# Two heads side by side in the two halves of the rows: sliding-window attention and mLSTM of a two-layer f32 block

## The chip, the cores and the metric

The kernel runs as one program on one core of a Trainium2 chip. The time is that of one execution on the device in microseconds; lower is better. The engines are PE (matmul; PEld is its weight load), DVE, ACT, POOL and SP, which issues DMAs. PE contracts over the partition dimension: a matmul's operands lie on up to 128 rows (partitions), and an operand of 64 rows may lie on rows 0 to 63 or on rows 64 to 127.

## The reference, cut to what matters

Two layers of feed-forward, token mixing, feed-forward and a gated embedding, then further blocks, on 512 rows of 1024. Within token mixing, these two parts matter here:

```python
# attention: 8 query heads over 2 key/value heads of 64, window 128, one sink logit per head
scores = jnp.einsum('bnqhgd,bnkhd->bnhgqk', qb, kb) * (HEAD_DIM ** -0.5)
scores = jnp.where(valid, scores, NEG_INF)
probs = jax.nn.softmax(jnp.concatenate([scores, sink], axis=-1), axis=-1)[..., :-1]
out = jnp.einsum('bnhgqk,bnkhd->bnqhgd', probs, vb)
...
# mLSTM: 4 heads of 64; C_t = f_t C_{t-1} + i_t v_t k_t^T, n_t = f_t n_{t-1} + i_t k_t,
# h_t = C_t q_t / max(|n_t . q_t|, 1), carried in a running-max (m) scaled form
h_m = mlstm_chunkwise(m_heads(q_m), m_heads(k_m), m_heads(v_m), i_pre, f_pre)
h_m = h_m * rsqrt(mean(h_m * h_m) + NORM_EPS) * mlstm_norm
y_mlstm = sigmoid(o_m) * h_m
y = jnp.concatenate([y_attn, y_mlstm, y_rwkv], axis=-1) @ w_out
```

## The kernel before

Activations are feature-major: tiles of 128 features x 512 rows of the sequence. Every weight product is a sum of three matmuls in a rounded format (operands split into a high part, names ending in h, and a low part, ending in l), accumulated in a PSUM bank named ps_ps. `mix` (once per layer) runs `lin_fm` over 22 tiles of w_mf; after each tile's 24 matmuls an evacuation function `evac` does the small work of the three token mixers. Tiles 16 to 21 are the queries, keys and values of the attention; behind tile 16 stands `ml_gates`, behind tile 21 the generator `attention` is started and then advanced by two steps in each of tiles 0 to 7, whose own work is the RWKV part; tiles 8 to 15 are the mLSTM's. Last come `ml_core` and the w_out product, whose operands are ymh and yml.

A scheduler of the framework orders each engine's instructions ahead of time; each engine then runs its queue in that order and waits at semaphores. PSUM has eight banks. In `mix`, `ps` has banks 0 and 1, `rw` 2 to 4, `at` 5 to 7; a call of `self.ps(shape, tag)` takes the tag's next bank in turn.

`attention` (L1072) loops over 4 blocks of 128 rows and, in each, over 4 steps i. A step is one half e of the rows (one key/value head; e = i // 2) and two of its query heads: scores of q and k over 64 rows (f32, each matmul two records in a profile) and the mask added by a bf16 product with an identity (m, id), the row maximum (mx), exponentials (pr, with their sum dn), the sink's exponential es, transposes of pr, a copy to pT, the product with v, and the division. A block's last step transposes the output (oo) back. Block 0 has 128 keys, the others 256.

`ml_gates` (L943) makes the gate rows: 16 rows x 512 (4 heads, each repeated 4 times) by scans, then splits them into Gh and Gl.

`ml_core` (L999) loops over 4 heads. Head h has its 64 features on rows 0 to 63 or 64 to 127 of tile j = h // 2. For each of four column blocks c (512, 384, 256, 128 columns wide) it broadcasts a gate row by two products of a selecting column `sel` with Gh and Gl over 16 rows, adds the triangular mask, takes the exponential (wt), multiplies k by q over 64 rows (mq in the profile, f32, two records), and multiplies both into pt. Ten products with va (64 columns and a column of ones) give the head's output; a chain of small ops (md, hh, msq, mms and the inverse root mly) normalises it. After each second head the two are transposed (hh), weighted (myg) and split (ymh, yml).

Of the kernel before, what the change touches and what calls it, by code (L numbers as in the profile page):

```python
# [10 lines left out]
F32 = mybir.dt.float32  # L11
# [46 lines left out]
NC1 = C_ROT + 128  # L58
# [8 lines left out]
def mixer_constants():  # L67
    c = np.zeros((P, NC1), np.float32)
    m = np.zeros((P, NM), np.float32)
    i = np.arange(P)  # L70
    m[:, M_UPS:M_UPS + P] = i[:, None] < i[None, :]
    m[:, M_UPI:M_UPI + P] = i[:, None] <= i[None, :]
    for n in range(7):
        b = 1 << n
        q = (i[:, None] // (2 * b) == i[None, :] // (2 * b)) & (i[:, None] % (2 * b) >= b) & (i[None, :] % (2 * b) < b)
        m[:, M_LEV + n * P:M_LEV + (n + 1) * P] = q
        if n == 0:
            m[:, M_LEV1T:M_LEV1T + P] = q.T
# [6 lines left out]
    cm = np.zeros((16, T), np.float32)  # L85
    for r in range(16):
        cm[r] = t >= P * (r // 4)
# [12 lines left out]
    return c, ca, c2, m, cm  # L100
# [11 lines left out]
class K:  # L112
# [830 lines left out]
    def ml_gates(self):  # L943
# [23 lines left out]
        pl = self.ps([16, NB, P], "rw")  # L967
        pi = self.ps([16, NB, P], "rw")
# [9 lines left out]
        cm = self.tmp("cm")[0:16, :]  # L978
# [6 lines left out]
        for b in range(NB):  # L985
            self.tr(pc[:, 0, b, :], I[:, b * P:(b + 1) * P])
            self.tr(pc[:, 1, b, :], M[:, b * P:(b + 1) * P])
# [5 lines left out]
        Gh, Gl = (pool.tile([16, T], F32R, name=n) for n in ("Gh", "Gl"))  # L993
        self.split(G, Gh, Gl)
        self.sel = pool.tile([16, 16], F32R, name="sel")
        nc.vector.tensor_copy(out=self.sel, in_=self.ident[0:16, 0:16])
        self.ml["gates"] = ac, em, Gh, Gl

    def ml_core(self, ys):  # L999

        nc, pool, ml = self.nc, self.pool, self.ml
        ac, em, Gh, Gl = ml["gates"]
        va = ml["va"]
        small = lambda nm, sh, bufs=2: pool.tile([P] + sh, F32, tag=nm, name=nm, bufs=bufs)
        for h in range(4):
            j, o = h // 2, (h % 2) * 64
            PT = []
            for c in range(NB):
                n = T - c * P
                rr = c * 4 + h  # L1010
                pw = self.ps([P, n], "at")
                sel = bc(self.sel[:, rr:rr + 1], [16, P])
# [3 lines left out]
                w = self.tmp("wt")[:, :n]  # L1016
                nc.scalar.activation(w, pw, AF.Exp, bias=ac[:, c, rr:rr + 1])
                s = self.ps([P, n], "rw")
                self.mm(s, ml[f"k{j}"][o:o + 64, c * P:(c + 1) * P], ml[f"q{j}"][o:o + 64, c * P:])
                pt = self.tmp("pt")[:, :n]  # L1020
                nc.vector.scalar_tensor_tensor(pt, s, 0.125, w, op0=ALU.mult, op1=ALU.mult)
                PT.append(pt)
            pn = self.ps([P, NB, 65], "at")
            for b in range(NB):
                for c in range(b + 1):
                    self.mm(pn[:, b, :], PT[c][:, (b - c) * P:(b - c + 1) * P], va[:, c, h, :], c == 0, c == b)
            den = small("md", [NB])
            nc.scalar.activation(den, pn[:, :, 64], AF.Abs)
            nc.vector.tensor_max(den, den, em[:, :, h])
            nc.vector.reciprocal(den, den)  # L1030
            if h % 2 == 0:
                hh = self.tmp("hh").rearrange("p (b a d) -> p b a d", a=2, d=64)
            hv = hh[:, :, h % 2, :]
            nc.vector.tensor_mul(hv, pn[:, :, 0:64], bc(den.unsqueeze(2), [P, NB, 64]))
            sq = small("msq", [NB, 64], 1)
            nc.scalar.activation(sq, hv, AF.Square)
            ms = small("mms", [NB])
# [3 lines left out]
            nc.vector.tensor_mul(hv, hv, bc(rs.unsqueeze(2), [P, NB, 64]))  # L1041
            if h % 2:
                pt = self.ps([P, NB, P], "rw")
                for b in range(NB):
                    self.tr(pt[:, b, :], hh[:, b, :, :].rearrange("p a d -> p (a d)"))
                yg = self.tmp("myg")
                nc.vector.scalar_tensor_tensor(yg, pt.rearrange("p a b -> p (a b)"), self.v(f"mnorm{self.l}", j), ml[f"og{j}"], op0=ALU.mult, op1=ALU.mult)
                self.split(yg, *ys[6 + j])
# [23 lines left out]
    def attention(self):  # L1072
# [5 lines left out]
        for j in range(4):  # L1078
            at[f"o{j}"] = at[f"q{j}"]
        for b in range(NB):  # L1080
# [3 lines left out]
            for i in range(4):  # L1084
                e, j0 = i // 2, 2 * (i % 2)
                o = slice(e * 64, e * 64 + 64)
                sc = self.ps([P, 2, 256], "at")
                for g in range(2):
                    ks = slice((b - 1 + k0) * P, (b + 1) * P)
                    dst = sc[:, g, k0 * P:]  # L1090
                    self.mm(dst, QT[j0 + g][o, sl], KT[o, ks], True, False)
                    self.mm(dst, self.id16, self.m16[:, k0 * P:256], False, True)
                mx = small("mx", [2])
                nc.vector.tensor_reduce(mx, sc[:, :, k0 * P:], axis=AX.X, op=ALU.max)
                sk = rb[:, so + 4 * e + j0:so + 4 * e + j0 + 2]
                nc.vector.scalar_tensor_tensor(mx, mx, 0.125, sk, op0=ALU.mult, op1=ALU.max)
                nc.vector.tensor_scalar(mx, mx, -1.0, None, op0=ALU.mult)
                dn = small("dn", [2])
                pr = self.tmp("pr").rearrange("p (a b) -> p a b", b=256)
                for g in range(2):  # L1100
                    nc.scalar.activation(pr[:, g, k0 * P:], sc[:, g, k0 * P:], AF.Exp, bias=mx[:, g:g + 1], scale=0.125,
                                         accum_out=dn[:, g:g + 1])
                es = small("es", [2])
# [4 lines left out]
                pp = self.ps([P, 2, 2, P], "at")  # L1108
                for g in range(2):
                    for kk in range(k0, 2):  # L1110
                        self.tr(pp[:, g, kk, :], pr[:, g, kk * P:(kk + 1) * P])
                pT = self.tmp("pT").rearrange("p (a b c) -> p a b c", b=2, c=P)
                nc.vector.tensor_copy(out=pT[:, :, k0:, :], in_=pp[:, :, k0:, :])
                po = self.ps([P, 2, 64], "at")
                for g in range(2):
                    for kk in range(k0, 2):
                        self.mm(po[:, g, :], pT[:, g, kk, :], vat[:, b - 1 + kk, e * 64:(e + 1) * 64], kk == k0, kk == 1)
                nc.vector.tensor_mul(oo.rearrange("p (h d) -> p h d", d=64)[:, 2 * i:2 * i + 2, :], po, bc(dn.unsqueeze(2), [P, 2, 64]))
                if i == 3:
# [913 lines left out]
```

## Time and profile before

| what | value |
|---|---|
| median of 3 runs | 4457.08 us (4456.84 to 4468.8) |
| the profiled execution | 4456.82 us, span 4454.9 us |
| PE busy | 4207.3 us, 94% |
| DVE, ACT, POOL busy | 2642.3 us (59%), 1613.4 us (36%), 845.6 us (19%) |
| granted TensorE clock, mean of the span | 0.955 |
| attention, first layer | within 449 to 565 us of the span |
| ml_core, first and second layer | 715.9 to 781.9 and 1985.3 to 2048.3 us |

The span is the profiled part; 1.9 us lie around it. A granted clock of 1 is 2.4 GHz, 0.5 is 1.2 GHz, and a value between is a mean over a stretch that had both. Matmuls overlap their neighbours in the pipeline, so what one costs is read from start to next start rather than from its duration.

### The profile page before, as it was taken

To read this page: it belongs to the slowest core of one execution; us is meant where nothing else is said; L and a number is where in the kernel's file an instruction comes from. 1 tells how busy PE (TensorE), PEld (TensorE's weight loads), DVE (VectorE), ACT (ScalarE), POOL (GpSimd) and SP (SyncE) were. 2 spreads that over 40 slices of the span, in tenths; PEclk is the share of its full clock that TensorE was granted. 3 is DMA by queue.
4 is the path that set the end of the run, shared out by engine and by line. 5 is a ranking of instruction groups with operands and counts; after the bars stand their busy time and mean duration, and the time that the engine had idled before them with its cause. 6 is when DMAs were issued, how large, how long until landed. Compare 5 with 4: busy or idle time off the path is not lost. (4 is left out here: it accounts for less than half of the span.)

```text
span 4454.9 us, 56951 instructions
## 1 busy us (share of the span) xinstructions
PE 4207.3 (94%) x21867; PEld 3559.3 (80%) x21867; DVE 2642.3 (59%) x5019; ACT 1613.4 (36%) x2542; POOL 845.6 (19%) x739
## 2 busy tenths in 40 slices
PE   8998999999999999999999889899878889999998
PEld 7887687888888886877888768788877878888887
DVE  4435664543464445645442766645667878777876
ACT  3223422432352233323332543443323743333332
POOL 0002210100110012111000332102655024333331
PEclk9999997999999999978999899899989999999999
DMA  3233100322332231002323310333444689899895
GB/s 122 99 93 123 48 11 29 122 96 95 128 114 99 96 126 58 25 29 78 106 95 115 129 59 29 118 129 132 166 148 170 251 311 328 308 322 323 312 318 184
DMA packets 234592, 628.71 MB, mean 141 GB/s; under 512 B 26800, under 2 KB 93488, under 8 KB 229968
## 3 DMA queue, kind: packets, MB, share of 16 engines
q1 hardware_dynamic: 195008, 464.11, 30.5%
q0 software_dynamic: 38736, 159.93, 10.1%
q8 instruction: 171, 2.80, 0.3%
q10 hardware_dynamic: 576, 1.05, 0.1%
q14 instruction: 101, 0.83, 0.1%
HBM read 562.06 MB, written 62.91 MB: 140 GB/s over the span
## 5 line engine op out<-in xcount | busy, mean ns | idle before, releaser
L193 PE MATMUL ps_ps<-xh,wl 128*128 128x512 f32 (+2 forms) x3568 | 1310.2, 368 | 53.0 <-DVE wl L184 52.8
L193 PE MATMUL ps_ps<-xl,wh 128*128 128x512 f32 (+2 forms) x3568 | 1315.8, 369 | 24.3 <-DVE xl L340 23.7
L193 PE MATMUL ps_ps<-xh,wh 128*128 128x512 f32 (+2 forms) x3568 | 1306.8, 368 | 33.0 <-ACT xh L348 12.6
L183 ACT CAST wh<-st 128x1024 fp32r<-128x1024 f32 (+1 forms) x560 | 580.0, 1038 | 1409.2 <-PE ps_ps L193 977.8
L184 DVE TENSOR_TENSOR wl<-st,wh 128x1024 fp32r<-128x1024 f32 (+1 forms) x496 | 600.2, 1211 | 431.2 <-ACT wh L183 430.3
L193 PEld LDWEIGHTS ps_ps<-xh,wl 128*128 128x128 f32 x3568 | 691.0, 194 | 147.1 <-DVE wl L184 60.1
L193 PEld LDWEIGHTS ps_ps<-xl,wh 128*128 128x128 f32 x3568 | 690.3, 194 | 118.5 <-DVE xl L340 35.2
L193 PEld LDWEIGHTS ps_ps<-xh,wh 128*128 128x128 f32 x3568 | 687.8, 193 | 119.0 <-ACT xh L348 14.0
L345 POOL TENSOR_TENSOR y<-y,x 128x256 f32<-128x256 f32 x64 | 54.7, 856 | 1756.0 <-DVE y L344 1515.3
L439 DVE TENSOR_TENSOR gu<-ps_ps,R 128x512 f32<-128x512 f32 x176 | 120.9, 691 | 450.1 <-PE ps_ps L193 449.4
L193 PE MATMUL ps_ps<-mh,wl 128*128 128x512 f32 (+1 forms) x920 | 327.8, 356 | 2.5 <-DVE wl L184 2.5
L193 PE MATMUL ps_ps<-mh,wh 128*128 128x512 f32 (+1 forms) x920 | 327.4, 356 | 1.2 <-DVE kf L1499 0.9
L193 PE MATMUL ps_po<-vh,ah 128*128 128x512 f32 x768 | 303.6, 397 | 25.8 <-ACT ah L1826 20.3
L193 PE MATMUL ps_po<-vh,al 128*128 128x512 f32 x768 | 303.9, 396 | 2.7 <-DVE al L1827 2.7
L193 PE MATMUL ps_po<-vl,ah 128*128 128x512 f32 x768 | 303.0, 394 | 0.3 <-DVE vl L1833 0.3
L193 PE MATMUL ps_ps<-ml,wh 128*128 128x512 f32 (+1 forms) x792 | 289.4, 365 | 0.0
L184 POOL TENSOR_TENSOR wl<-st,wh 128x1024 fp32r<-128x1024 f32 x64 | 155.8, 2437 | 242.3 <-ACT wh L183 225.9
L1767 POOL DMA_INDIRECT rows<-in_pv_dram,idx x128 | 175.1, 1368 | 117.0 <-DVE acc L1790 109.3
L193 PEld LDWEIGHTS ps_ps<-mh,wl 128*128 128x128 f32 x920 | 174.9, 190 | 26.7 <-DVE wl L184 2.7
L193 PEld LDWEIGHTS ps_ps<-mh,wh 128*128 128x128 f32 x920 | 174.8, 190 | 25.8 <-DVE kf L1499 1.1
L193 PEld LDWEIGHTS ps_po<-vh,ah 128*128 128x128 f32 x768 | 146.7, 191 | 58.7 <-ACT ah L1826 24.4
L193 PEld LDWEIGHTS ps_po<-vh,al 128*128 128x128 f32 x768 | 145.9, 190 | 38.9 <-DVE al L1827 8.3
(700 smaller groups left out, 6199.6 us busy)
## 6 DMA issues: line engine op xcount, KB each, us to landing
st<-in_pu_dram SPq DMA_DIRECT2D x128, 512.0 KB, 4.7
vst<-in_pv_dram SPq DMA_DIRECT2D x128, 512.0 KB, 5.8
st<-in_w1i_dram SPq DMA_DIRECT2D x88, 512.0 KB, 3.4
st<-in_w2i_dram SPq DMA_DIRECT2D x88, 512.0 KB, 3.4
G<-gst POOLq DMA_DIRECT2D x12, 2048.0 KB, 8.2
gt<-G SPq DMA_DIRECT2D x384, 64.0 KB, 5.1
st<-in_wmf_dram SPq DMA_DIRECT2D x44, 512.0 KB, 3.5
xd<-y SPq DMA_DIRECT2D x20, 1024.0 KB, 3.8
```

Source lines behind the costliest of these rows:

```text
L183: nc.scalar.copy(out=wh[:, :n], in_=st[:, :n])
L184: self.wl_eng.tensor_sub(wl[:, :n], st[:, :n], wh[:, :n].bitcast(F32))
L193: i = self.nc.tensor.matmul(out, lhsT=lhsT, rhs=rhs, start=start, stop=stop)
L345: nc.gpsimd.tensor_add(y[k + 1], y[k + 1], self.xin[k + 1][:, c])
L439: nc.vector.tensor_mul(t, psum, R)
L1767: self.nc.gpsimd.indirect_dma_start(out=t, out_offset=None, in_=self.d["pur" if w == "u" else "pvr"], in_offset=bass.IndirectOffsetOnAxis( ...
```

## The change

`attention` loops over two steps per block instead of four: a step does two query heads of both halves, with the score products of the halves alternating and each half in a bank of its own; maxima, sums and the division are made for all four heads at once, over the same columns of one output bank. `evac` advances the generator once per tile instead of twice. `ml_core` loops over two pairs of heads: products of the two halves alternate, and the normalising ops work on both heads at once. The gate row's high and low parts lie in one tile Gs, so that one product over 64 rows (16 of high, 16 empty, 16 of low, 16 empty) gives what Gh and Gl gave by two; Gs repeats on rows 64 to 127. `ml_gates` therefore makes its rows on 128 partitions, with a larger constant cm and 16 more columns in C. The number of DMAs is the same.

```diff
-                    for _ in range(2):
-                        next(att, None)
+                    next(att, None)
...
-                rep = pool.tile([P, 4, 4], F32, tag="grep", name="grep", bufs=4)
-                nc.vector.tensor_copy(out=rep, in_=bc(src[:, b, :].unsqueeze(1), [P, 4, 4]))
+                rep = pool.tile([P, 4, 32], F32, tag="grep", name="grep", bufs=4)
+                nc.gpsimd.memset(rep[:, :, 16:32], 0.0)
+                nc.vector.tensor_copy(out=rep[:, :, 0:16].rearrange("p q (a b) -> p q a b", b=4),
+                                      in_=bc(src[:, b, :].unsqueeze(1).unsqueeze(1), [P, 4, 4, 4]))
...
-        LF, I, M, G = (self.tmp(n)[0:16, :] for n in ("LF", "I", "M", "G"))
+        LF, I, M, G = (self.tmp(n) for n in ("LF", "I", "M", "G"))
...
-        Gh, Gl = (pool.tile([16, T], F32R, name=n) for n in ("Gh", "Gl"))
-        self.split(G, Gh, Gl)
+        Gs = pool.tile([P, T], F32R, name="Gs")
+        nc.scalar.copy(out=Gs, in_=G)
+        for o in (32, 96):
+            nc.vector.tensor_sub(Gs[o:o + 32, :], G[o:o + 32, :], Gs[o:o + 32, :].bitcast(F32))
...
-        for h in range(4):
-            j, o = h // 2, (h % 2) * 64
+        rows = (slice(0, 64), slice(64, 128))
+        for j in range(2):
...
-                self.mm(pw, sel, Gh[:, c * P:], True, False)
-                self.mm(pw, sel, Gl[:, c * P:], False, False)
-                self.mm(pw[:, 0:P], self.id16, self.m16[:, 256:384], False, True)
...
-                self.mm(s, ml[f"k{j}"][o:o + 64, c * P:(c + 1) * P], ml[f"q{j}"][o:o + 64, c * P:])
+                for e, o in enumerate(rows):
+                    rr = c * 4 + 2 * j + e
+                    self.mm(pw[e], bc(self.sel[o, rr:rr + 1], [64, P]), Gs[o, c * P:], True, False)
+                s = [self.ps([P, n], "rw") for _ in range(2)]
+                for e, o in enumerate(rows):
+                    self.mm(s[e], ml[f"k{j}"][o, c * P:(c + 1) * P], ml[f"q{j}"][o, c * P:])
+                for e in range(2):
+                    rr = c * 4 + 2 * j + e
+                    self.mm(pw[e][:, 0:P], self.id16, self.m16[:, 256:384], False, True)
...
-            sq = small("msq", [NB, 64], 1)
-            nc.scalar.activation(sq, hv, AF.Square)
+            nc.vector.tensor_max(den, den, em[:, :, 2 * j:2 * j + 2])
             nc.vector.reciprocal(den, den)
+            for e in range(2):
+                nc.vector.tensor_mul(hh[:, :, e, :], pns[e][:, :, 0:64], bc(den[:, :, e:e + 1], [P, NB, 64]))
+            sq = self.tmp("msq").rearrange("p (b a d) -> p b a d", a=2, d=64)
+            nc.scalar.activation(sq, hh, AF.Square)
...
-            for i in range(4):
-                e, j0 = i // 2, 2 * (i % 2)
-                o = slice(e * 64, e * 64 + 64)
-                sc = self.ps([P, 2, 256], "at")
+            for j0 in (0, 2):
+                sc = [self.ps([P, 2, 256], "at") for _ in range(2)]
+                ks = slice((b - 1 + k0) * P, (b + 1) * P)
                 for g in range(2):
-                    ks = slice((b - 1 + k0) * P, (b + 1) * P)
-                    dst = sc[:, g, k0 * P:]
-                    self.mm(dst, QT[j0 + g][o, sl], KT[o, ks], True, False)
-                    self.mm(dst, self.id16, self.m16[:, k0 * P:256], False, True)
+                    for e, o in enumerate(rows):
+                        self.mm(sc[e][:, g, k0 * P:], QT[j0 + g][o, sl], KT[o, ks], True, False)
+                    for e in range(2):
+                        self.mm(sc[e][:, g, k0 * P:], self.id16, self.m16[:, k0 * P:256], False, True)
...
+                for e in range(2):
+                    for g in range(2):
+                        nc.scalar.activation(pr[e][:, g, k0 * P:], sc[e][:, g, k0 * P:], AF.Exp, bias=mx[:, e, g:g + 1], scale=0.125,
+                                             accum_out=dn[:, e, g:g + 1])
```

In the rows of the order below, a line is the kernel's line (three more in the changed kernel), then the operation, its output and operands with their buffer numbers, and the shape of the output. PE at the start of ml_core in the first layer, before:

```order
L193 MATMUL ps_at_5462<-Gh_3113,sel_3117 128x512
L193 MATMUL ps_at_5462<-Gl_3114,sel_3117 128x512
L193 LDWEIGHTS id16_2877
L193 MATMUL ps_at_5462<-m16_2879,id16_2877 128x128
L193 MATMUL ps_rw_5468<-mq_4749,mq_5041 128x512
L193 MATMUL ps_at_5472<-Gh_3113,sel_3117 128x384
L193 MATMUL ps_at_5472<-Gl_3114,sel_3117 128x384
```

And with the change, at the same place:

```order
L196 MATMUL ps_at_5387<-Gs_3121,sel_3125 128x512
L196 MATMUL ps_at_5388<-Gs_3121,sel_3125 128x512
L196 MATMUL ps_rw_5391<-mq_4669,mq_4961 128x512
L196 MATMUL ps_rw_5392<-mq_4669,mq_4961 128x512
L196 LDWEIGHTS id16_2877
L196 MATMUL ps_at_5387<-m16_2879,id16_2877 128x128
L196 LDWEIGHTS id16_2877
L196 MATMUL ps_at_5388<-m16_2879,id16_2877 128x128
L196 MATMUL ps_at_5403<-Gs_3121,sel_3125 128x384
L196 MATMUL ps_rw_5407<-mq_4669,mq_4961 128x384
L196 LDWEIGHTS id16_2877
L196 MATMUL ps_at_5403<-m16_2879,id16_2877 128x128
```

The gate rows of two heads (two banks) now stand next to each other, and so do the two k-q products; at the 384-wide block the second head's gate row and product stand later, behind six products of w_out.

PE at the first scores of the attention (block 0, first layer), before:

```order
L193 MATMUL ps_ps_3284<-xh_2630,wl_3287 128x512
L193 MATMUL ps_at_3361<-qk_3236,qk_2998 128x128
L193 LDWEIGHTS id16_2877
L193 MATMUL ps_at_3361<-m16_2879,id16_2877 128x128
L193 MATMUL ps_at_3361<-qk_3236,qk_3119 128x128
```

And with the change:

```order
L196 MATMUL ps_ps_3292<-xh_2630,wl_3295 128x512
L196 MATMUL ps_at_3369<-qk_3244,qk_2998 128x128
L196 MATMUL ps_at_3370<-qk_3244,qk_2998 128x128
L196 LDWEIGHTS id16_2877
L196 MATMUL ps_at_3369<-m16_2879,id16_2877 128x128
L196 LDWEIGHTS id16_2877
L196 MATMUL ps_at_3370<-m16_2879,id16_2877 128x128
L196 MATMUL ps_at_3369<-qk_3244,qk_3127 128x128
L196 MATMUL ps_at_3370<-qk_3244,qk_3127 128x128
```

Score products of the two halves stand next to each other, into two banks. At the first step of block 1 they don't:

```order
L196 MATMUL ps_at_3605<-qk_3244,qk_2998 128x256
L196 MATMUL ps_rw_3549<-C_2844,ksq_3547 128x2 x4
L196 LDWEIGHTS id16_2877
L196 MATMUL ps_at_3605<-m16_2879,id16_2877 128x256
L196 MATMUL ps_at_3605<-qk_3244,qk_3127 128x256
L196 LDWEIGHTS id16_2877
L196 MATMUL ps_at_3605<-m16_2879,id16_2877 128x256
L196 MATMUL ps_ps_3656<-xl_2631,wh_3658 128x512
L212 MATMUL ps_at_3501<-io_75,oo_3368 128x128 x3
L196 MATMUL ps_at_3606<-qk_3244,qk_2998 128x256
```

Here the first half's two products with their masks come first, then the last block's output transposes, and only then the second half.

## Rows read from the trace of the kernel before

**Rows 1.** Windows: length, busy (count) of PE, PEld, DVE, ACT, POOL; clock; DMA.

```profile
460.00:560.00 100.00, 97.48 (x482) 69.31 (x481) 65.13 (x174) 43.42 (x118) 22.35 (x28) 0.97 0.12 43
715.90:781.90 66.00, 65.63 (x217) 42.80 (x216) 23.75 (x78) 16.88 (x31) 0.00 (x0) 0.64 0.03 8
1985.30:2048.30 63.00, 62.63 (x217) 41.37 (x216) 23.69 (x78) 16.89 (x31) 0.00 (x0) 0.67 0.03 9
```

**Rows 2.** Timeline of PE in ml_core, first layer: start, duration, instruction, count, [idle before].

```profile
715.93 0.49 PE L193 MATMUL ps_at<-Gh,sel 16*128 16x512 f32 x1
716.27 0.38 PE L193 MATMUL ps_at<-Gl,sel 16*128 16x512 f32 x1
716.59 0.23 PE L193 MATMUL ps_at<-m,id 128*128 128x128 bf16 x1
716.75 1.12 PE L193 MATMUL ps_rw<-mq 64*128 64x512 f32 x2
717.80 0.44 PE L193 MATMUL ps_at<-Gh,sel 16*128 16x384 f32 x1
...
746.72 2.07 PE L193 MATMUL ps_rw<-mq 64*128 64x512 f32 x2
...
773.19 0.77 PE L193 MATMUL ps_ps<-ymh,wh 128*128 128x512 f32 x1
...
778.91 0.39 PE L193 MATMUL ps_ps<-ymh,wh 128*128 128x512 f32 x1
779.14 0.60 PE L209 MATMUL ps_rw<-io,hh 128*128 128x128 f32 x4
...
780.58 0.50 PE L193 MATMUL ps_ps<-ymh,wh 128*128 128x512 f32 x1 [0.37 <-DVE myg L1047]
```

**Rows 3.** Windows of PE in ml_core and in the attention: busy time, clock.

```profile
735.00:745.00 10.00, 10.00 (x34) 0.50 0.01 2
510.00:520.00 10.00, 10.00 (x37) 0.66 0.16 54
```

**Rows 4.** Timeline of PE in the RWKV chain, first layer, columns as in rows 2.

```profile
632.81 0.27 PE L193 MATMUL ps_rw<-rt,bt 64*128 64x128 f32 x1
632.81 0.27 PE L193 MATMUL ps_rw<-at,kt 64*128 64x128 f32 x1
```

**Rows 5.** Windows of PE in the RWKV chain: one half alone, then both halves.

```profile
631.48:632.03 0.55, 0.55 (x5) 1.00 0.00 0
632.03:632.93 0.90, 0.90 (x17) 1.00 0.00 0
```

**Rows 6.** Timeline of PE in the attention: scores of 128 and of 256 columns.

```profile
459.96 0.48 PE L193 MATMUL ps_at<-qk 64*128 64x128 f32 x2
460.38 0.23 PE L193 MATMUL ps_at<-m,id 128*128 128x128 bf16 x1
...
501.05 0.70 PE L193 MATMUL ps_at<-qk 64*128 64x256 f32 x2
501.68 0.28 PE L193 MATMUL ps_at<-m,id 128*128 128x256 bf16 x1
```

**Rows 7.** Waits of PE from 460 to 560: total, times, longest.

```profile
PE ps_at L193 <- DVE pT L1113: 1.3, 1, 1.3
PE ps_rw L193 <- DVE us L714: 0.6, 1, 0.6
```

**Rows 8.** Groups of DVE and ACT, 460 to 565: busy, mean ns, idle before.

```profile
L1094 DVE TENSOR_REDUCE mx<-ps_at 128x2 f32<-128x512 f32 x10 | 6.9, 686 | 2.3 <-PE ps_at L193 2.3
L1101 ACT ACTIVATE pr<-ps_at,mx 128x256 f32<-128x256 f32 x18 | 8.4, 477 | 10.5 <-DVE mx L1097 10.5
```

**Rows 9.** Groups of DVE in ml_core, first layer, columns as in rows 8.

```profile
L1021 DVE SCALAR_TENSOR_TENSOR pt<-ps_rw,wt 128x512 f32<-128x512 f32 x4 | 2.8, 688 | 2.4 <-PE ps_rw L193 1.5 <-ACT wt L1017 0.8
L1034 DVE TENSOR_TENSOR hh<-ps_at,md 128x256 f32<-128x256 f32 x4 | 1.7, 424 | 0.4
```

**Rows 10.** Timeline of DVE in ml_gates, first layer.

```profile
437.20 0.67 DVE L983 TENSOR_TENSOR I<-I,G 16x512 f32<-16x512 f32 x1
```

More of the change, by code (lines that the diff above doesn't have):

```diff
@@ L84, in mixer_constants @@
     t = np.arange(T)
-    cm = np.zeros((16, T), np.float32)
-    for r in range(16):
-        cm[r] = t >= P * (r // 4)
+    cm = np.zeros((P, T), np.float32)
+    for r in range(P):
+        if r % 32 < 16:
+            cm[r] = t >= P * (r % 32 // 4)
+            c[r, C_S16 + r % 32] = 1.0
     c[:, C_HI] = i < 64
@@ L999, in ml_core @@
+        self.sel = pool.tile([P, 16], F32R, name="sel")
+        nc.vector.tensor_copy(out=self.sel, in_=self.C[:, C_S16:C_S16 + 16])
+        self.ml["gates"] = ac, em, Gs
     def ml_core(self, ys):
         nc, pool, ml = self.nc, self.pool, self.ml
-        ac, em, Gh, Gl = ml["gates"]
+        ac, em, Gs = ml["gates"]
         va = ml["va"]
         small = lambda nm, sh, bufs=2: pool.tile([P] + sh, F32, tag=nm, name=nm, bufs=bufs)
-        for h in range(4):
-            j, o = h // 2, (h % 2) * 64
-            PT = []
+        rows = (slice(0, 64), slice(64, 128))
@@ L1008, in ml_core @@
+        for j in range(2):
+            PT = [[], []]
+            own = [[self.tmp("pt"), self.tmp("pt")] for _ in range(2)]
+            both = self.tmp("pt")
             for c in range(NB):
                 n = T - c * P
-                rr = c * 4 + h
-                pw = self.ps([P, n], "at")
-                sel = bc(self.sel[:, rr:rr + 1], [16, P])
-                self.mm(pw, sel, Gh[:, c * P:], True, False)
-                self.mm(pw, sel, Gl[:, c * P:], False, False)
-                self.mm(pw[:, 0:P], self.id16, self.m16[:, 256:384], False, True)
@@ L1037, in ml_core @@
-            ms = small("mms", [NB])
+                pw = [self.ps([P, n], "at") for _ in range(2)]
+                for e, o in enumerate(rows):
[7 more added lines that the diff above has]
+                    self.mm(pw[e][:, 0:P], self.id16, self.m16[:, 256:384], False, True)
+                    w = self.tmp("wt")[:, :n]
+                    nc.scalar.activation(w, pw[e], AF.Exp, bias=ac[:, c, rr:rr + 1])
+                    pt = (own[e][0], own[e][1][:, :n], both[:, e * 256:(e + 1) * 256], own[e][1][:, 384:])[c]
+                    nc.vector.scalar_tensor_tensor(pt, s[e], 0.125, w, op0=ALU.mult, op1=ALU.mult)
+                    PT[e].append(pt)
@@ new lines, in ml_core @@
+            den = small("md", [NB, 2])
+            hh = self.tmp("hh").rearrange("p (b a d) -> p b a d", a=2, d=64)
+            pns = []
+            for e in range(2):
+                pn = self.ps([P, NB, 65], "at")
+                for b in range(NB):
+                    for c in range(b + 1):
+                        self.mm(pn[:, b, :], PT[e][c][:, (b - c) * P:(b - c + 1) * P], va[:, c, 2 * j + e, :], c == 0, c == b)
+                nc.scalar.activation(den[:, :, e], pn[:, :, 64], AF.Abs)
+                pns.append(pn)
@@ L1040, in ml_core @@
             rs = self.rsqrt_small(pool, ms, "ml")
[L1041 to L1048, printed above, removed]
+            nc.vector.tensor_mul(hh, hh, bc(rs.unsqueeze(3), [P, NB, 2, 64]))
+            pt = self.ps([P, NB, P], "rw")
+            for b in range(NB):
+                self.tr(pt[:, b, :], hh[:, b, :, :].rearrange("p a d -> p (a d)"))
+            yg = self.tmp("myg")
+            nc.vector.scalar_tensor_tensor(yg, pt.rearrange("p a b -> p (a b)"), self.v(f"mnorm{self.l}", j), ml[f"og{j}"], op0=ALU.mult, op1=ALU.mult)
+            self.split(yg, *ys[6 + j])
     def at_tile(self, i, psum):
@@ L1103, in attention @@
-                es = small("es", [2])
+                dn = small("dn", [2, 2])
+                pr = [self.tmp("pr").rearrange("p (a b) -> p a b", b=256) for _ in range(2)]
+                for e in range(2):
+                    for g in range(2):
+                        nc.scalar.activation(pr[e][:, g, k0 * P:], sc[e][:, g, k0 * P:], AF.Exp, bias=mx[:, e, g:g + 1], scale=0.125,
+                                             accum_out=dn[:, e, g:g + 1])
+                es = small("es", [2, 2])
@@ L1107, in attention @@
                 nc.vector.reciprocal(dn, dn)
[L1108 to L1119, printed above, removed]
+                pT = []
+                for e in range(2):
+                    pp = self.ps([P, 2, 2, P], "at")
+                    for g in range(2):
+                        for kk in range(k0, 2):
+                            self.tr(pp[:, g, kk, :], pr[e][:, g, kk * P:(kk + 1) * P])
+                    pT.append(self.tmp("pT").rearrange("p (a b c) -> p a b c", b=2, c=P))
+                    nc.vector.tensor_copy(out=pT[e][:, :, k0:, :], in_=pp[:, :, k0:, :])
+                po = self.ps([P, 2, 2, 64], "at")
+                for e in range(2):
+                    for g in range(2):
+                        for kk in range(k0, 2):
+                            self.mm(po[:, e, g, :], pT[e][:, g, kk, :], vat[:, b - 1 + kk, e * 64:(e + 1) * 64], kk == k0, kk == 1)
+                nc.vector.tensor_mul(oo.rearrange("p (e h d) -> p e h d", e=2, d=64)[:, :, j0:j0 + 2, :], po, bc(dn.unsqueeze(3), [P, 2, 2, 64]))
+                if j0:
                     pt = self.ps([P, 4, P], "at")
```

48 lines of the change are left out of this document (14 added, 34 removed).

## The prediction

> **What bounds the kernel now.** I read the two stretches that the change rewrites first by the view that gives each engine's busy time in a window. In the attention of the first layer PE is busy 97.48 of 100 us, DVE 65 and ACT 43; in ml_core it is busy 65.63 of 66 us in the first layer and 62.63 of 63 in the second, DVE and ACT about a third and a quarter of it [rows 1]. So both stretches end with PE's own work, and any PE time that leaves them shortens the kernel until another engine is late. The second thing to see is the granted clock: 0.97 in the attention, but 0.64 and 0.67 in ml_core, that is, large parts at 1.2 instead of 2.4 GHz. Granted clock times busy time gives the work of ml_core at full clock: 65.63 x 0.64 and 62.63 x 0.67, 42.0 us in both layers. Some 24 and 21 us of it are the price of the low clock.
>
> The timeline of PE then shows what runs there. One head's widest step is Gh 0.34 us (start to next start, 715.93 to 716.27), Gl 0.32, the mask 0.16, and the product of k and q 1.05 [rows 2]; the same product takes 2.07 later, at the low clock [rows 2]. In the ten microseconds from 735, all gate rows, masks and k-q products, the clock is 0.50 with PE never idle [rows 3]. These products fill 16 or 64 of the 128 rows of the array (the shapes of rows 2 say so). Right behind dense 128-row products, at 716, the clock is still full.
>
> **Do the halves overlap?** The change bets on this, and the trace of before has it once, in the RWKV chain, where products on rows 0 to 63 and on rows 64 to 127 are neighbours in PE's queue. There a row of each half starts at the same 632.81 [rows 4], and 17 matmul records start in 0.90 us where one half alone starts 5 in 0.55 [rows 5]: 0.053 against 0.11 us each. Two neighbouring products on the two halves cost about one. Products of one half, or with anything else between them, don't.
>
> **Part 1, ml_core.** By PE's new order, the same in both layers, not all pairs are neighbours. Of the eight pairs of k-q products five are: 512 and 256 wide for the first two heads, 512, 384 and 128 for the others. Prices at full clock: 512 wide 1.05 [rows 2]; 128 wide 0.42, from the attention product of that shape [rows 6]; 0.63 and 0.84 between by interpolation. Saved: 1.05 + 0.63 + 1.05 + 0.84 + 0.42 = 4.0 us. Four of the eight gate-row pairs are neighbours, at most 0.34 each and less for narrow ones: about 1.1. The sixteen Gl products go: 0.32 for the widest, I take 0.26 on average: 4.2. Together 9.3 of 42.0 us at full clock, 32.7 stay.
>
> New waits on PE. The tail of two heads is one chain now, and its ops are twice as wide: reduce, square and last multiply go from 256 to 512 columns, from 0.42, the price of a 256-wide multiply there [rows 9], to about 0.69, that of a 512-wide reduce [rows 8], so 0.27 each, and one more such 0.42 multiply by the denominator: 1.2 us longer. At the end of the last two heads sixteen w_out products of 0.23 us (778.91 to 779.14 [rows 2]) cover it, 3.7 us. The old chain took at most 773.19 to 779.14, 5.95 us [rows 2], since hh began without a wait there; so PE waits between 0 and 3.4 us, and I take 1.8. Behind it in PE's queue stand the transposes of hh and then the rest of w_out, which needs the rows that myg makes: some 2 us more, of which 0.37 were there before [rows 2]. For the first two heads twelve w_out products, the next gate rows and k-q products cover the chain; but there the whole tail stands on DVE ahead of the first two multiplies (pt) of the next heads, 0.69 each [rows 9], which free the banks of the next k-q products: about 1 us. Waits together 5 us, with 3 and 8 as ends. The second og table load, which sat between exponentials on ACT, is gone: nothing, as PE didn't wait there.
>
> So ml_core takes 32.7 us divided by the granted clock, plus 5. Which clock? The pairs fill all 128 rows for the first time, Gl is gone, and the stretch keeps its dense w_out products, as the attention does that runs at 0.97 [rows 1]; but unpaired ones, 65-column products and a wait remain, and after a wait of 0.6 us [rows 7] the attention itself fell to 0.66 for ten microseconds [rows 3]. I take 0.88: 37.2 + 5 = 42 us instead of 66 and 63, **-24 and -21, -45 us**. At 1.0 and with waits of 3 it is -57 (35.7 us a layer), at 0.5 throughout +8 (65.4 + 3, since a slow PE hides more).
>
> By the Trainium skill, "TensorE: Matmul & The Clock Gate", section on HAM oscillation, it is waits between groups of matmuls that throw PE back to the slow clock. The trace does not agree here: PE waits 0.37 us in 66 and is granted 0.64. If the page's rule alone held, fuller rows would give no clock back, which is rival 1 below.
>
> **Part 2, attention.** A 256-wide score product takes 0.63 us (501.05 to 501.68), a 128-wide one 0.42 [rows 6]; a layer has 24 and 8, twelve and four pairs. In the new order all four narrow pairs are neighbours and seven of the wide ones; in blocks 1 and 2 the rest are split, since a bank or a mask comes between. Saved per layer: 7 x 0.63 + 4 x 0.42 = 6.1 us. The softmax chain of a step doubles: two reduces of 0.69, four exponentials of 0.48 instead of two [rows 8], some 2 us longer before the transposes may start, and the casts of the next weights stand behind it on ACT. Half as many chains run, and in most steps a whole tile of 24 w_mf products (5 us) lies between scores and transposes; in block 1 seven do, 1.6 us. Before, PE's longest wait there was 1.3 us for pT [rows 7]. New waits 0 to 4 us a layer. Fewer changes between 64- and 128-row products give back up to 1. I take 6.1 saved, 0.9 gained, 1 lost: **-6 per layer, -12**.
>
> **Part 3, gates.** cm and C are loaded 8 times and a few per cent larger, both ahead of their use; the widened scans and copies keep their 512 columns, so their time. New on the path are eight small POOL memsets and, at the end, two subtractions over 32 rows for one over 16; such an op is 0.67 us [rows 10]. The gate rows are read some 280 us later [rows 2, 10]. Bounds 0 and 2 us, taken **+0.5 per layer, +1**.
>
> **Sum.** -45 - 12 + 1 = -56 on the profiled execution's 4456.8 us (span 4454.9 and 1.9 around it), which lies 0.3 below the median of the three runs: **4401 us**.
>
> **Rivals.** 1. *The clock stays low.* For it: the same kinds of products, new waits, and the attention's own fall. Against: rows are paired, and Gl, the emptiest, is gone. With the old 0.655, 32.7 / 0.655 + 5 = 55 us, -11 and -8; at 0.58, 61 us, -5 and -2; the attention and gates add -11. 4427 to 4439, say 4434.
> 2. *The halves don't overlap* for these products (the shown pair is 128 wide, not 512). Then only Gl goes: 4.2 / 0.655 = 6.4 us a layer less 5 of waits, and the attention loses what it gains: about 4455.
> 3. *Slower: pairs run PE out of banks.* Scores, transposes and outputs share three banks, a step now holds two at once, and PE's in-order queue stands behind the first that isn't free. 16 steps in two layers, each w us longer: with the clock low as in rival 1 the rest of the change gives -7 - 14 + 1 = -20, so from w = 1.25 us the kernel is slower, and at 2.4 us, the chain's whole added length and a stretch at half clock behind it, it is 4457 - 20 + 38 = 4475. For it: 0.6 us of wait already cost a slow stretch [rows 3]. Against: DVE is a third free, ACT more [rows 1], and the order places products between. The Trainium skill, "TensorEngine Tiling (Array Packing)", restrictions, PSUM pressure, says that different row tiles need different banks; the code gives each half its own, and no row here prices the lack.
>
> **How the numbers follow.** Forecast 0.62, a larger gain (full clock, below 4387) 0.06, rival 1 0.2, rival 2 0.07, rival 3 0.05. The range runs from the full clock with short waits, 4457 - 57 - 14 + 1 = 4387, to rival 1's slow end, 4439; rivals 2 and 3, the gain below it and the tail of rival 1 stay out, under 0.2. About 0.3%, 13 us, is what a measurement of this kernel tells from no change: faster takes forecast, larger gain and most of rival 1, 0.84; the same the rest of it and most of rival 2, 0.11; slower 0.05.
>
> **What would show it.** In the new timeline: equal starts of the two k-q rows of a pair (else rival 2); granted clock over ml_core near 0.9 and its length near 42 us (near 0.6 and 60: rival 1); PE waits in the attention stretch below 4 us (some 20: rival 3); a wait of 1 to 3 us ahead of hh and another behind it. Wrong by much would be a clock that falls after those waits into the w_out products, and the rest of w_out with it.

## The result

The changed kernel takes 4407.04 us (median of 4 runs, 4401.27 to 4422.05), the kernel before 4457.24 us on the same chip: ratio 0.9894, 95% interval 0.9871 to 0.9916, 50 us less by the medians. A second timing with five executions gave 0.9882 (0.9859 to 0.9906). Every ratio below is to the kernel before on the same chip. The forecast was 4401 us with a range of 4387 to 4439.

The page of the profile after: the span is 51 us shorter, PE's busy time 70 us. In the clock strip ml_core lies in the seventh and the eighteenth slice, which held 7 and 7 before and hold 9 and 8 now; most of such a slice of 110 us is other work.

```profile
span 4403.7 us, 56669 instructions
PE 4137.3 (94%) x21835; PEld 3513.9 (80%) x21835; DVE 2627.9 (60%) x4873; ACT 1609.7 (37%) x2522; POOL 852.8 (19%) x755
PEclk9999989999999998989999899999898999999999
```

To compare kernels I cut each layer's mixing into two stretches. **Stretch A** runs from one and the same w_mf product, just behind the start of w_mf, to the first gate row of ml_core: it holds the gates, the attention and the RWKV chain. **Stretch M** runs from the first gate row to the last transposes of hh. Windows of PE; the columns are window, length, PE busy (records), granted clock, DMA share and rate; A and M of the first layer, then of the second. Before:

```profile
392.41:715.94 323.53, 309.69 (x1783) 0.95 0.13 45
715.94:779.48 63.54, 63.54 (x209) 0.62 0.03 9
1662.56:1985.36 322.80, 313.26 (x1729) 0.91 0.12 41
1985.36:2045.82 60.46, 60.46 (x209) 0.66 0.03 9
```

After:

```profile
389.80:714.98 325.18, 309.21 (x1784) 0.93 0.13 45
714.98:749.99 35.01, 32.95 (x195) 1.00 0.05 16
1631.46:1950.28 318.82, 305.43 (x1730) 0.91 0.12 42
1950.28:1985.38 35.10, 32.93 (x195) 1.00 0.04 16
```

M is 28.5 and 25.4 us shorter, 54 in sum, a little more than the span's whole 51; A is 2.3 us shorter in sum, and the rest of the kernel is 5 us longer. In M the clock is 1.00 where it was 0.62 and 0.66. (The prediction's ml_core [rows 1] ends some 2.5 us later than M, with the next products of w_out; by those ends it takes 37.6 and 37.7 us after the change.)

The timeline of PE at the start of M after, where rows 2 stood before. Four records of k and q, two heads, take 0.95 us up to the next product (715.31 to 716.26); one head's two took 1.05 [rows 2]. The product with va, 40 records, runs at full clock, 4.68 us, and at the end PE waits twice.

```profile
714.97 0.50 PE L196 MATMUL ps_at<-Gs,sel 64*128 64x512 f32 x2
715.31 1.02 PE L196 MATMUL ps_rw<-mq 64*128 64x512 f32 x4
716.26 0.28 PE L196 MATMUL ps_at<-m,id 128*128 128x128 bf16 x2
...
723.56 4.68 PE L196 MATMUL ps_at<-va,pt 128*128 128x65 f32 x40
...
749.61 0.66 PE L212 MATMUL ps_rw<-io,hh 128*128 128x128 f32 x4 [1.82 <-DVE hh L1055]
751.11 0.50 PE L196 MATMUL ps_ps<-ymh,wh 128*128 128x512 f32 x1 [0.84 <-DVE myg L1060]
```

### The profile page after: what moved, and what is told of

The parts are those of the page before. It is cut to its first block, busy times and chain, and to the rows that moved or that the text cites. A ratio compares the mean times of both kernels' runs of the same rounds, so it can differ in the third digit from the quotient of the medians.

```text
span 4403.7 us, 56669 instructions
## 1 busy us (share of the span) xinstructions
PE 4137.3 (94%) x21835; PEld 3513.9 (80%) x21835; DVE 2627.9 (60%) x4873; ACT 1609.7 (37%) x2522; POOL 852.8 (19%) x755
## 3 DMA queue, kind: packets, MB, share of 16 engines
q10 hardware_dynamic: 576, 1.05, 0.1%
## 5 line engine op out<-in xcount | busy, mean ns | idle before, releaser
L196 PEld LDWEIGHTS ps_ps<-xh,wh 128*128 128x128 f32 x3568 | 686.4, 193 | 117.9 <-ACT wh L186 13.4
```

Source lines behind the costliest of these rows:

```text
L196: i = self.nc.tensor.matmul(out, lhsT=lhsT, rhs=rhs, start=start, stop=stop)
```

## The experiments

My theory after the result was the prediction's: overlapping halves shorten the work and, by filling all rows, bring the clock back. The rival was that the clock came back for another reason, and the overlap is a bystander. Where no interval is given below, the kernel ran once, and its time is one execution's.

**Each part alone.** `ml_only` takes ml_gates, ml_core and the constants of the change with the attention before, `att_only` the reverse.

> Only the mLSTM part of the change (gate rows in one tile, ml_core with two heads side by side); the attention is the one before. If the whole gain sits in ml_core, as the two traces suggest (66 and 63 us before, 37.6 and 37.7 after), ml_core takes 37 to 38 us at a granted clock of 1.0 in both layers, and the time is 4403 to 4409 us, within 4 us of the full change apart from what the last stages scatter. Rival, the attention brought part of it: 4412 us or more.

> Only the attention's part of the change; gates and ml_core are those before. If the attention gains its 6 us a layer but gives most of it back as new waits and lower clock, the stretch from the start of w_mf to ml_core is 1 to 4 us shorter than the 316 and 312 us of before in sum over both layers, ml_core keeps 63 to 66 us at a clock of 0.64 to 0.67, and the time is 4452 to 4457 us. Rival, the forecast's 6 us a layer: 4445 us.

`ml_only`: 4398.87 us, ratio 0.987 (0.9834 to 0.9905). `att_only`: 4452.51 us, 0.9991 (0.9973 to 1.0008). The gain sits in ml_core. M of `ml_only` in both layers:

```profile
719.18:754.21 35.03, 32.94 (x194) 1.00 0.05 16
1956.90:1991.92 35.02, 32.95 (x194) 1.00 0.05 16
```

Stretches A and M of `att_only`, as above:

```profile
390.70:712.52 321.82, 305.78 (x1782) 0.94 0.14 46
712.52:772.97 60.45, 60.45 (x208) 0.66 0.03 9
1649.80:1970.57 320.77, 306.75 (x1728) 0.91 0.12 41
1970.57:2029.58 59.01, 59.01 (x208) 0.68 0.03 10
```

**Without the overlap, in ml_core.** `ml_seq` is `ml_only` with one half's products ahead of the other's, a mask between them:

```diff
                 pw = [self.ps([P, n], "at") for _ in range(2)]
+                s = [self.ps([P, n], "rw") for _ in range(2)]
                 for e, o in enumerate(rows):
                     rr = c * 4 + 2 * j + e
                     self.mm(pw[e], bc(self.sel[o, rr:rr + 1], [64, P]), Gs[o, c * P:], True, False)
-                s = [self.ps([P, n], "rw") for _ in range(2)]
-                for e, o in enumerate(rows):
                     self.mm(s[e], ml[f"k{j}"][o, c * P:(c + 1) * P], ml[f"q{j}"][o, c * P:])
-                for e in range(2):
-                    rr = c * 4 + 2 * j + e
                     self.mm(pw[e][:, 0:P], self.id16, self.m16[:, 256:384], False, True)
```

> As the mLSTM part alone, but within each column block first one half's gate row, k-q product and mask, then the other's, so that the halves are hardly ever neighbours; instructions and work are the same. Theory A, pairs that overlap both save 5 us of work and bring the clock back: granted clock 0.6 to 0.75 in ml_core and 52 to 60 us. Rival B, the clock came back because the Gl products over 16 rows are gone: clock 0.95 to 1.0 and about 43 us.

> The mLSTM part alone with the halves one after the other, timed in rounds. If the overlap of the halves is worth its 4 us of work a layer, it is 6 to 8 us slower than the mLSTM part with pairs (0.987 of before), ratio near 0.989; if that work is spent on waits, the ratio is the same within 0.001, and its stretch from the first gate row to the last transposes is 36 us at a clock of 1.0 again.

The clock stays at 1.00 with nearly no neighbours left (the order of the queue still makes a few), and the kernel is no slower: 4406.39 us in one execution and, in four more, 4391.67 us, 0.9868 (0.9852 to 0.9885). Theory A falls: it had 52 to 60 us at 0.6 to 0.75. Rival B had the clock right and put the length at 43 us. M of the first and the second layer, from the four:

```profile
718.83:754.75 35.92, 35.45 (x195) 1.00 0.04 16
1945.44:1981.37 35.93, 35.46 (x195) 1.00 0.05 16
```

PE is busy 2.5 us longer than with pairs, but M is only 0.9 us longer, because the waits ahead of hh shrink from 2.0 us to 0.5. PE's wait for hh from 700 to 800 us of this run, total, times, longest:

```profile
PE ps_rw L212 <- DVE hh L1053: 0.5, 1, 0.5
```

and from the first gate row to 755 us of the full change:

```profile
PE ps_rw L212 <- DVE hh L1055: 2.0, 2, 1.8
```

**What the gate row does to the clock.** Three kernels keep the heads of `ml_only` side by side and change the gate row alone: `ml_gl` makes it by Gh and Gl over 16 rows, as before (for it and `hi16` ml_gates is the old one too); `hi16` by Gh alone, leaving the low part out; `two64` by two products over 64 rows. The first diff is `ml_gl`, of which `hi16` keeps the first product only; the second is `two64`.

```diff
-                    self.mm(pw[e], bc(self.sel[o, rr:rr + 1], [64, P]), Gs[o, c * P:], True, False)
+                    sel = bc(self.sel[:, rr:rr + 1], [16, P])
+                    self.mm(pw[e], sel, Gh[:, c * P:], True, False)
+                    self.mm(pw[e], sel, Gl[:, c * P:], False, False)
```

```diff
-                    self.mm(pw[e], bc(self.sel[o, rr:rr + 1], [64, P]), Gs[o, c * P:], True, False)
+                    for i in range(2):
+                        self.mm(pw[e], bc(self.sel[i][o, rr:rr + 1], [64, P]), Gs[o, c * P:], i == 0, False)
```

> As the mLSTM part alone, but each gate row again by two products, Gh and Gl, over 16 rows on rows 0 to 15, for each head; the k-q products stay side by side. Theory A (filled rows in the k-q pairs keep the clock): some 5 to 6 us more work, granted clock above 0.85, 43 to 48 us. Rival B (the 16-row products are what lowers the clock): clock 0.6 to 0.75, 55 us or more.

> As the mLSTM part alone, heads side by side, but the gate row is the single product Gh over 16 rows; the low part Gl is left out, so the output is less exact. As many gate products as in the change, over 16 rows instead of 64. If the rows that a product fills decide, the clock is below 0.85 in ml_core and it takes 44 us or more; if the number of products in the stretch decides, the clock is 1.0 and ml_core takes 37 to 39 us.

> As the mLSTM part alone, heads side by side, but each gate row by two products over 64 rows, one selecting the high part and one the low; as many products as with Gh and Gl, over 64 rows instead of 16. If rows decide: clock 0.95 to 1.0, 40 to 44 us. If the number of products decides: as with Gh and Gl, clock near 0.8 and 52 us.

M of both layers. `ml_gl` (4438.77 us):

```profile
720.20:772.14 51.94, 51.94 (x210) 0.70 0.03 11
1963.96:2017.33 53.37, 53.37 (x210) 0.68 0.03 10
```

`hi16` (4417.22 us):

```profile
725.11:773.45 48.34, 47.41 (x194) 0.72 0.04 12
1961.98:2003.21 41.23, 41.15 (x194) 0.83 0.04 14
```

`two64` (4429.31 us):

```profile
721.85:769.05 47.20, 47.15 (x210) 0.71 0.03 12
1960.42:2007.78 47.36, 47.31 (x210) 0.71 0.04 12
```

Both simple answers fail. One product over 16 rows instead of 64 loses the clock for a part of M, and so does a second product over 64 rows. All six stretches lost it, though one layer of `hi16` only to 0.83; of the fourteen stretches with this loop and one product over 64 rows (`ml_only`, `ml_seq` twice, the full change twice, `att_seq` and `att_split`), thirteen were at 1.00 and one at 0.87.

Which product brings the fall is not shown. In the first layer of `hi16` the first block of gate rows still runs at full clock, and the products with va behind it (40 records, 65 columns each) take nearly twice as long:

```profile
735.00 8.62 PE L196 MATMUL ps_at<-va,pt 128*128 128x65 f32 x40
743.55 0.79 PE L196 MATMUL ps_at<-Gh,sel 16*128 16x512 f32 x1
```

8.62 us against 4.68 after the change; the next gate row then takes 0.79 instead of 0.49. But in its second layer that block takes 4.68 us as well, and the clock falls only some 26 us behind the first gate row, in a k-q product. In the other five stretches it falls 9.0 to 10.5 us behind the first gate row: inside the products with va in three, ahead of them in both layers of `ml_gl`. In the kernel before it falls 2.8 us behind the first gate row (3.2 in the second layer), in a k-q product, with no product of va yet. Windows of PE ahead of the fall and behind it, as above: `ml_gl`, second layer, up to its first products with va at 1975.29 and through them,

```profile
1963.96:1972.96 9.00, 9.00 (x39) 1.00 0.19 60
1972.96:1983.97 11.01, 11.01 (x51) 0.50 0.00 0
```

and the kernel before, first layer, whose first product with va stands at 729.11:

```profile
715.94:718.69 2.75, 2.75 (x10) 1.00 0.00 0
718.69:728.94 10.25, 10.25 (x25) 0.51 0.16 52
```

**The single gate product in the old loop.** `one_gate` is the kernel before with that product alone; `one_gate2` also puts the k-q product ahead of the mask. The first diff is `one_gate`, in the loop over single heads, the second what `one_gate2` has besides.

```diff
-                self.mm(pw, sel, Gh[:, c * P:], True, False)
-                self.mm(pw, sel, Gl[:, c * P:], False, False)
+                self.mm(pw, bc(self.sel[o:o + 64, rr:rr + 1], [64, P]), Gs[o:o + 64, c * P:], True, False)
```

```diff
+                s = self.ps([P, n], "rw")
+                self.mm(s, ml[f"k{j}"][o:o + 64, c * P:(c + 1) * P], ml[f"q{j}"][o:o + 64, c * P:])
                 self.mm(pw[:, 0:P], self.id16, self.m16[:, 256:384], False, True)
-                s = self.ps([P, n], "rw")
-                self.mm(s, ml[f"k{j}"][o:o + 64, c * P:(c + 1) * P], ml[f"q{j}"][o:o + 64, c * P:])
```

> The kernel before with one thing taken from the change: the gate row is one product of Gs over the 64 rows of the head's own half instead of two over 16 rows; heads, tails and order stay those of before, one head after the other, and the attention too. Theory B (the 16-row products lower the clock): ml_core at a clock above 0.9, 42 to 46 us instead of 66 and 63, total near 4415 us. Rival C (two heads side by side are needed, for the overlap or for the order that comes with it): clock 0.65 to 0.75, 55 to 61 us, total 4440 to 4450.

> As the kernel before with the single gate product over 64 rows, one head after the other, but the k-q product stands right behind the gate row, on the same half, and the mask after both. If what one_gate still lacked was the alternation of 64-row and 128-row products, ml_core now keeps a clock above 0.95 and its last transposes come within 38 us of its first gate row; if it lacked the pairing of heads, the clock stays at 0.84 to 0.89 and 46 to 48 us.

`one_gate`: 4425.8 us, 0.9933 (0.9905 to 0.996). M:

```profile
716.98:764.88 47.90, 45.16 (x194) 0.84 0.04 12
1962.05:2007.98 45.93, 43.20 (x194) 0.89 0.04 12
```

`one_gate2`, 4419.93 us in one run:

```profile
724.82:762.97 38.15, 37.88 (x194) 1.00 0.05 15
1959.94:2002.64 42.70, 42.43 (x194) 0.88 0.04 13
```

So the gate product alone gives 15.6 and 14.5 us of M's 28.5 and 25.4, with heads one after the other; the ratio 0.9933 says the same 30 us. With the mask behind the k-q product M is another 9.8 and 3.2 us shorter. In each layer 2.5 us of that is PE's wait for hh at the end of M, 2.7 us in `one_gate` and 0.3 here; the rest, 7.3 us in the first layer, goes with its clock, 0.84 to 1.00. The full clock came in one layer and not in the other: neither theory of that expectation is borne out. As this is one execution, and the full change too lost its clock in one stretch (below), what the mask's place does to the clock is not shown. The timeline of `one_gate2` shows one part of what the new order saves, whose counterpart in rows 2 is the 1.05: right behind a gate row of the same half the k-q product costs 0.94 (725.20 to 726.14). The head takes 1.44 us up to the next gate row (724.86 to 726.30), where it took 0.34 + 0.32 + 0.16 + 1.05 = 1.87 before [rows 2].

```profile
724.86 0.49 PE L196 MATMUL ps_at<-Gs,sel 64*128 64x512 f32 x1
725.20 1.02 PE L196 MATMUL ps_rw<-mq 64*128 64x512 f32 x2
726.14 0.23 PE L196 MATMUL ps_at<-m,id 128*128 128x128 bf16 x1
726.30 0.43 PE L196 MATMUL ps_at<-Gs,sel 64*128 64x384 f32 x1
```

**The attention.** `att_seq` is the full change with one half's scores and masks ahead of the other's. `att_split` keeps the paired scores but gives each half, behind them, a chain of its own as before the change (maxima, exponentials, transposes, output).

```diff
 # att_seq
-                for g in range(2):
-                    for e, o in enumerate(rows):
-                        self.mm(sc[e][:, g, k0 * P:], QT[j0 + g][o, sl], KT[o, ks], True, False)
-                    for e in range(2):
-                        self.mm(sc[e][:, g, k0 * P:], self.id16, self.m16[:, k0 * P:256], False, True)
+                for e, o in enumerate(rows):
+                    for g in range(2):
+                        self.mm(sc[e][:, g, k0 * P:], QT[j0 + g][o, sl], KT[o, ks], True, False)
+                        self.mm(sc[e][:, g, k0 * P:], self.id16, self.m16[:, k0 * P:256], False, True)
```

`att_split`, cut to the chain's head:

```diff
-                mx = small("mx", [2, 2])
-                for e in range(2):
-                    nc.vector.tensor_reduce(mx[:, e, :], sc[e][:, :, k0 * P:], axis=AX.X, op=ALU.max)
...
+                for e in range(2):
+                    mx = small("mx", [2])
+                    nc.vector.tensor_reduce(mx, sc[e][:, :, k0 * P:], axis=AX.X, op=ALU.max)
...
+                    po = self.ps([P, 2, 64], "at")
```

> The full change, but in the attention the products of one half come first with their masks, then the other half's, so that no two halves are neighbours. Forecast: the pairs save 6 us of PE work a layer; then PE's busy time times clock between the start of w_mf and ml_core rises by 5 to 6 us a layer against the full change. If that saving is spent on waits, the length of the stretch rises by 2 us or less; if it counts, by 5 to 6.

> The full change, but behind the paired score products each half has a softmax chain, transposes and output of its own, as before the change. If the doubled chain makes the new waits, PE's idle time between the start of w_mf and ml_core falls from 16 and 13 us to the 10 to 14 of before and the two stretches together are 5 us or more shorter than the change's 644 us; if the three banks do, the idle time stays, and pairs stand apart in the order.

A of both layers, `att_seq` (4410.44 us):

```profile
391.09:723.09 332.00, 320.53 (x1782) 0.92 0.13 45
1639.81:1952.18 312.37, 303.43 (x1728) 0.95 0.13 43
```

`att_split` (4409.42 us):

```profile
391.70:721.09 329.39, 314.79 (x1784) 0.92 0.13 45
1637.54:1956.64 319.10, 308.46 (x1730) 0.91 0.13 42
```

Busy time times clock is PE's work at full clock. The full change has 287.6 and 277.9 us of it in A, `att_seq` 294.9 and 288.3: the pairs do save 7 and 10 us, a little more than forecast. The lengths don't follow: 644.0 us in sum with pairs, 644.4 without. By the two kernels' lines PE idles 11.5 and 8.9 us in A without pairs and 16.0 and 13.4 with them, so 9.0 of the 17.7 us saved come back as waits; the other part goes with a clock of 0.93 and 0.91 where `att_seq` had 0.92 and 0.95. A layer's A alone can't be read: where its attention is the old one, its length went from 323.5 to 333.5 us in the first layer and from 308.7 to 322.8 in the second, with the clock. The sum of both layers is steadier: 638 to 649 us, mean 643.7, over the nine runs with the old attention (before, `ml_only`, `ml_seq` twice, `one_gate`, `one_gate2`, `hi16`, `two64`, `ml_gl`), and 644.0, 642.6 and 637.5 in the three of the change's attention (full, `att_only`, full again): 2 us less, inside the scatter.

Before the change PE idled 13.8 and 9.5 us in A. The new waits are not on the softmax but on RWKV products beside it, whose operands DVE, ACT and POOL make (first layer, total, times, longest; rows 7 held 0.6 for the first of them):

```profile
PE ps_rw L196 <- DVE us L716: 2.5, 2, 1.7
PE ps_rw L212 <- POOL kt L705: 1.4, 2, 0.7
PE ps_rw L196 <- ACT ksq L675: 1.3, 1, 1.3
PE ps_rw L212 <- DVE us L634: 1.1, 1, 1.1
```

With chains of their own (`att_split`) the idle time falls to 14.6 and 10.6, part of the way that the theory of the doubled chain had it, and the work stays small (289.6 and 280.7), but A is 648.5 us in sum, at a clock of 0.92 and 0.91, where that theory had it 5 us shorter than 644. So the doubled chain is at most a part. The clock is 0.925 on average in the six stretches with the change's attention (0.91 to 0.94), 0.937 in the eighteen with the old one (0.91 to 0.96). On some 288 us of work that is 4 us a layer. Whether the change lowers the clock there or these stretches happened to get less of it can't be told from so few, and stays open.

**The full change again**, in five executions:

> The full change once more, in more rounds, beside the mLSTM part alone (ratios 0.987 and 0.9868 to before). If the attention's part is worth its forecast 12 us, the ratio is near 0.984; if it is worth nothing, 0.986 to 0.990. In both layers the stretch from the first gate row to the last transposes is again 35 us at a clock of 1.0, and the two stretches ahead of it are 641 to 647 us together.

0.9882 (0.9859 to 0.9906): no faster than the mLSTM part alone (0.987 and, without pairs, 0.9868). M of both layers:

```profile
717.48:752.50 35.02, 32.95 (x195) 1.00 0.05 16
1946.89:1985.78 38.89, 36.98 (x195) 0.87 0.05 15
```

The second layer's M lost its clock for a part this once, 9.8 us behind its first gate row and within the products with va; the other nine stretches M with paired heads and one gate product over 64 rows (the full change, `ml_only`, `att_seq`, `att_split`) were at 1.00. A in sum was 637.5 us, below the 641 to 647 expected. The lowest ratio is that of the mLSTM part without neighbours, but its interval meets those of the full change and of `ml_only`, so which of the three is fastest is not shown.

## Why the prediction came true, point by point

- **Bound.** PE ended both stretches before, and in M its time turned into the kernel's almost one to one: busy 30.6 and 27.5 us less, length 28.5 and 25.4. Right for ml_core; in the attention new waits took half of what PE saved.
- **Overlap.** Rival 2 is out: four records start in the time of two, in ml_core (0.95 us) and in the attention (0.43 us from 456.05 for the first four score records of 128 columns, where two took 0.42 [rows 6]). But its worth in the time was misjudged twice. In M the pairs save 2.5 us of PE's busy time (35.45 to 32.95), not 5.1, since `ml_seq` keeps a few neighbours and its k-q products are cheaper behind a gate row than behind a mask; and of the 2.5 only 0.9 shorten M, as the chain on DVE comes last there.
- **Gl and the work of ml_core.** The widest Gl product costs its 0.32: `one_gate2`'s head is 0.43 shorter than that of before, 0.11 of it in the k-q product. Over the whole of M busy time times clock was 39.4 and 39.9 (63.54 x 0.62, 60.46 x 0.66) and is 32.95, so 6.5 and 7.0 went, where the forecast had 9.3; by the prediction's own ends 42.0 became 34.7, 7.3 less. The measure is rough where the clock is low (`one_gate`, without Gl, has 37.9 and 38.4 by it, and 37.9 in `one_gate2` at a clock of 1.00), so the 4.2 of the sixteen Gl products is neither shown nor refuted.
- **Waits in ml_core.** 2.0 ahead of hh and 0.8 behind it, 2.8 us instead of 5; the 1 us foreseen ahead of the second pair's k-q products did not come.
- **Clock.** The term that carries the result: 1.00 where I took 0.88, and with the shorter waits this made ml_core, by the prediction's ends, 37.6 and 37.7 us instead of 42 and the layers' gain 54 instead of 45 us. Of the reasons given for it the first, pairs that fill all rows, was wrong: without neighbours the clock is as high, and with them but a second or a 16-row gate product it is 0.68 to 0.83. The second, that Gl is gone, holds in part: `one_gate`, which takes the two products over 16 rows away and pairs nothing, has 0.84 and 0.89. No single property decides: of the gate rows tried only the single product over 64 rows kept 1.00, and in the old loop in one stretch of four. So the size of the clock term was a judgement that came out near, not a mechanism understood. The working also misread one row: the ten microseconds from 735 [rows 3] are gate rows, masks and k-q products only up to 740.89, and products with va, 20 records, behind.
- **Attention.** The step that failed: -12 us became about -2. The saved work was sized right (6 to 7 us a layer forecast, 7 to 10 found); the new waits were put at 1 us a layer and are 2 to 4 against before (4.5 against `att_seq`), on RWKV products that I hadn't named; and the lower clock that came with the rest wasn't in the sum. The 0.9 us a layer for fewer changes between 64- and 128-row products was not measured by itself.
- **Gates.** +1 us can't be seen in the scatter of A.
- **Rivals 1 and 3.** The clock didn't stay low in M. Banks cost no 20 us in the attention, but waits did take the place of work there, as rival 3 had it, though PE waited for operands of RWKV products. No run tests the banks by themselves.

The total fits by luck: a gain in ml_core that was 9 us too small met one in the attention that was 10 us too large. The 5 us by which the profiled execution missed the forecast lie outside A and M.

By the Trainium skill, "TensorE: Matmul & The Clock Gate", section on HAM oscillation, long waits between groups of matmuls, there for DMAs, bring the slow clock. The trace has a slow clock without them: before the change PE is busy through all of M at 0.62 and 0.66. The waits after it, 2.0 us in the first layer's M at a clock of 1.00, are shorter than those that the page tells of and don't speak against it.

## What to carry to other kernels

Where PE is busy all the time and its granted clock is low, look at what the products are and not only at waits: merging two small-row products into one over more rows gave 0.7% of this kernel by itself, most of it through the clock (the stretch's work at full clock went from 39.4 to 37.9 us, its length from 63.5 to 47.9), and can be tried alone before any regrouping of loops. Why the clock answers to it stays open. Products of two halves of the rows do run at once, but saved PE work is only time if PE doesn't then wait for other engines; here the version without overlap is as fast. Judge such a change by PE's work (busy time times clock), idle time and length of one stretch, since the total hides two errors that cancel.

## What the runs showed of the hardware

- The granted clock fell to 1.2 GHz while PE was busy with hardly a gap, 2.8 us behind the first gate row in the kernel before (715.94 to 718.69 at 1.00, 0.51 behind), and 9.0 to 10.5 us behind it in five of the six stretches of `ml_gl`, `hi16` and `two64`. It fell in k-q products and masks as well as in the 65-column products with va; those took 8.62 us for 40 records in the first layer of `hi16`, 7.58 and 8.74 in `two64` and `ml_gl`, 4.68 with the clock kept.
- Two k-q products on the two halves, neighbours in the queue, take 0.95 us for four records, as long as one alone behind a gate row of its half (0.94).
- A k-q product of 64 rows and 512 columns costs 0.94 us (`one_gate2`) to 0.95 (`ml_seq`) behind a gate row of the same half and 1.05 behind a 128-row mask (before).
- Stretch A took 323.5 to 333.5 us in the first layer and 308.7 to 322.8 in the second with nearly the same instructions, with PE's work (busy time times clock) at 293.6 to 295.9 in the first layer and 285.1 to 288.5 in the second, and the granted clock between 0.91 and 0.96. This is of the kernels with the old attention.
